# The first MLP's first chunk run for each token half apart, and the second half's norm queued behind the first half's products

## The chip, the cores and the metric

The kernel runs on one core of a Trainium2 chip. The metric is device microseconds (us) of one execution, as the median of several runs. In the profile PE is the matrix engine, PEld its weight load, DVE the vector engine, ACT the scalar engine, POOL the GpSimd engine, and SP the queue that issues the DMAs.

## What is computed

One inference step of two layers over 640 tokens of 1024 channels: 128 context tokens and 512 latent tokens. The part of the reference around the change, cut to what matters:

```python
xs = xs + m_lat[2] * ms                                      # token mixer's output, through w_out
hs = rmsnorm(xs, norm_mlp[i]) * (1.0 + m_lat[4]) + m_lat[3]   # norm and modulation
xs = xs + m_lat[5] * sqrelu_mlp(hs, mlp_w1[i], mlp_w2[i])     # square(relu(h @ w1)) @ w2, 1024 -> 4096 -> 1024
```

The context tokens take the same steps with their own modulation vectors. Layer 0 mixes tokens by a bidirectional linear recurrence, layer 1 by a convolution module (a matrix product with a gate, 31 taps along the tokens, a LayerNorm and another matrix product). The modulation vectors of a layer are one matrix product of a conditioning vector.

## The kernel before

**Layout.** Channels lie on the 128 partitions in eight tiles, tokens along the row. The tokens are worked in two halves of 320, called half 0 and half 1 here; the tiles of half 0 are `a` (input of a product) and `c` (hidden layer), those of half 1 `b` and `d`. Every operand is split in two parts (`h`, the rounded value, and `l`, the rest), and every product is made of three: `wh*ah` (L178), `wl*ah` (L181), `wh*al` (L182).

**Units.** A unit is one weight tile of 128 outputs and 1024 inputs against one half: 8 x 3 = 24 products into one PSUM tile `ps_mm`, of which there are three in turn (pool `mmp`, L79). For each weight tile `fetch` (L154) issues a DMA, an ACT cast (`wh`, L161) and a subtraction (`wl`, L163); line 162 says whether DVE or POOL does the subtraction, by the place of the tile in the list `plan`: POOL for the tiles of `w_out` and of the first MLP's chunk 0 and for a long stretch of layer 1, and in between (both_n to busy) POOL and DVE in turn. Weights are fetched three units ahead.

**The MLP.** The hidden layer of 4096 is worked in four chunks of 1024. `mlp_in` makes eight units and evacuates each by an ACT relu, a DVE multiplication (`hr`, L702), an ACT cast (`ch`, `dh`, L167) and a DVE subtraction (`cl`, `dl`, L168); `mlp_out` makes eight units whose results DVE adds to the residual stream `xr` (L285). The last product of the first `mlp_out` unit needs the last `cl` of the chunk.

**Background.** `bg` is a list of small steps of other work, each with a price in us; after every unit `between` (L193) hands out steps up to `budget[1]`. `drain` empties the list at once, or up to a mark. Two kinds of steps stand in it here. A norm of a half (L270): eight squares on ACT with DVE additions (`nacc`, L255), column sums on PE (`ps_n`, L236 or L228), the root and its inverse (`rc`, `rs`), a second set of PE products that spread it (L240), and eight times a multiplication (`nt`, L276), a modulation (L268 or ACT L266) and a split. And the 96 steps of layer 1's modulation (`mod_steps`, L115): 48 DMAs of 512 KB into three buffers `wm`, each read by two DVE instructions (`scratch`, L128) that multiply 1024 columns and sum them up.

**Order.** A scheduler puts the instructions of each engine in a fixed order, close to that of the code; an engine then works strictly through its own list. Before the change, the first MLP goes like this: `w_out` for half 0, then for half 1, with each half's norm queued behind it; `drain()` empties the list; then chunk 0 for both halves in groups of four units (32 units, budget 1.8), and chunks 1 to 3 for half 0 alone (48 units, budget 1.2), with the modulation steps behind them. What is called pass A here is that work of half 0. Pass B follows (L840 to L849): half 1's chunks 1 to 3, with the first matrix product of the convolution module for half 0 after five units, and the convolution of half 0 as background (budget 2.4). Then comes `pw2(0)`, the convolution module's last product for half 0, with half 1's next norm behind it.

Of the kernel before, what the change touches and what calls it, by code (L numbers as in the profile page):

```python
# [17 lines left out]
D = 1024  # L18
# [28 lines left out]
CA = 5  # L47
# [22 lines left out]
def hybrid_step(ctx: ExitStack, tc: tile.TileContext, xt, vec, pos, masks, ident_in, state, c_rows, w_mod0, w_modt,  # L70
# [25 lines left out]

# [1 line left out]
    mod = const.tile([P, 2, 48, 2], F32, name="mod")  # L98
    amod = const.tile([P, 2, 2, KT, 2], F32, name="amod")

    def mod_done(layer, j, src):
        """Adds the bias to chunks 2j and 2j+1, and for a chunk that scales makes norm_w * (1 + scale)."""
        bm = ap(vt, VEC["b_mod"].start + layer * 48 + j * 16, [[4, 4], [1, 4], [0, 2]])
        dst = ap(mod, (layer * 48 + j * 16) * 2, [[8, 4], [2, 4], [1, 2]])
        dve.tensor_tensor(dst, src, bm, ALU.add)
        for which in range(2):
            if j != (0, 2)[which]:
                continue
            base = (layer * 48 + (8, 32)[which]) * 2
            nw = VEC[("norm_mix", "norm_mlp")[which]].start + layer * 8  # L110
            dve.scalar_tensor_tensor(
                amod[:, layer, which].rearrange("p k s -> p (k s)"), ap(mod, base, [[1, 16]]), 1.0,
                ap(vt, nw, [[1, 8], [0, 2]]), ALU.add, ALU.mult)

    def mod_steps(cbs, raw_m, scratch, layer, j0, wm):  # L115
        """Chunks from 2 * j0 on of a layer's modulation, as dot products along rows of the transposed weights."""
        for s in range(2):
            cr = raw.tile([P, D], F32, tag="rw", name="cr")
            sync.dma_start(cr[:], c_rows[s:s + 1].partition_broadcast(P))
            act.activation(cbs[:, s], cr[:], AF.Sigmoid)  # L120
            dve.tensor_tensor(cbs[:, s], cbs[:, s], cr[:], ALU.mult)
        box = {}

        def step(i, s):
            if s == 0:
                box["w"] = wm()
                sync.dma_start(box["w"][:], w_modt[layer * 32 + i - 16 * (1 - layer)])
            tc.keep_in_program_order(dve.scalar_tensor_tensor(  # L128
                scratch, box["w"][:], 1.0, cbs[:, s], ALU.mult, ALU.mult, accum_out=raw_m[:, i, s:s + 1]))
            if s == 1 and i % 16 == 15:  # L130
                mod_done(layer, i // 16, ap(raw_m, (i - 15) * 2, [[8, 4], [2, 4], [1, 2]]))

        return [lambda i=i, q=q: step(i, q) for i in range(16 * j0, 48) for q in range(2)]
# [3 lines left out]

# [1 line left out]
    MLP = [[[w_mlp[l, c, u] for u in range(16)] for c in range(4)] for l in range(2)]  # L139
    PW1 = [w_pw1[u] for u in range(16)]  # L140
    PW2 = [w_pw2[u] for u in range(8)]
    plan = [w_in[u] for u in range(40)] + [w_out[u] for u in range(8)] * 2
    plan += MLP[0][0]
    both_n = len(plan)
    plan += MLP[0][1] + MLP[0][2] + MLP[0][3]
    busy = len(plan)
    plan += MLP[0][1][:CA] + PW1 + MLP[0][1][CA:] + MLP[0][2] + MLP[0][3] + PW2 + PW1
    plan += MLP[1][0] + MLP[1][1] + MLP[1][2] + PW2
# [59 lines left out]
    def linear(n, acts, evac, cols, group=8, after=between, u0=0, done=None):  # L208
        """n units of weights against the token halves given in cols: {half: (lo, hi)}."""
        first = pos_w[0]  # L210
# [11 lines left out]

# [1 line left out]
    def inv_rms(tp, acc, n, by_token):  # L224
        """1/rms of the columns of acc, the squares summed along D but for the partitions, on all partitions."""
        ps = axp.tile([P, 512], F32, tag="ax", name="ps_n")
# [17 lines left out]
    def rms_stat(tp, xs, n, by_token=False):  # L244
        """Steps that leave 1/rms over the KT tiles xs(k) in the returned box."""
        box = {}
# [53 lines left out]

# [1 line left out]
    h = {0: new_act("a"), 1: new_act("b")}  # L302
    first_ps = [[(mmp, "mm"), (scp, "sc")][half][0].tile([P, 512], F32, tag=("mm", "sc")[half], name=f"ps_f{half}")
                for half in (0, 1) for _ in range(3)]
    with tc.tile_pool(name="start", bufs=1) as st:
# [26 lines left out]

        # shift and scale in blocks of columns, so that the first products start with the first block
        wmb = {}
# [83 lines left out]
        sync.dma_start(vt[:, n0:], vec[:, n0:])  # L418
        # forget gate lower bounds: softmax over the layer axis, cumulated, less the first row
        lbt = const.tile([P, 16], F32, name="lbt")  # L420
# [40 lines left out]
    with tc.tile_pool(name="wm0", bufs=1) as wmp, tc.tile_pool(name="hd", bufs=1) as hd:  # L461
# [33 lines left out]
        def blocks(x, y, evac, w=SB, other=False):  # L495
            """Scores within blocks of w tokens (or across two neighbours), source token on the partition."""
            ps = scp.tile([P, 512], F32, tag="sc", name="ps_sc")
# [8 lines left out]
        def decay(hs, li):  # L506
            """Keeps the operands of a level aside and takes the running products one level up."""
            lv = LEVELS[li]
# [34 lines left out]
        def score(hs, li):  # L543
            """li < 0: equal tokens; else the pairs that part at that level."""
            if li < 0:
# [109 lines left out]

# [1 line left out]
    xpool = ctx.enter_context(tc.tile_pool(name="xpool", bufs=1))  # L657
# [37 lines left out]

# [1 line left out]
    def hid_evac(hid):  # L697
# [16 lines left out]
    def mlp_out(layer, cols, group=8, done=None):  # L714
        linear(8, hid, residual(xr, layer, 5), cols, group, done=done)

    def start_norm(layer, which, half, cols, first=True, by_token=False, on_dve=ND):
        """Queues a norm of one token half; returns its last step."""
        h[half] = new_act("ab"[half])
        steps = norm_steps(tp, xr, layer, which, h[half], *cols, by_token, on_dve)  # L720
        bg[:] = steps + bg if first else bg + steps
        return steps[-1]
# [4 lines left out]

    # w_out, then the first MLP; the first token half runs ahead of the second
    budget[1] = 3.0
    for cols in (A0, B0):  # L730
        linear(8, on, residual(xr, 0, 2), cols, done=lambda half: start_norm(0, 1, half, COLS[0][half], False, TM0, ND0))
    drain()
    with tc.tile_pool(name="wm1", bufs=1) as wmp:
# [3 lines left out]
            lambda: wmp.tile([P, D], F32, tag="wm", name="wm", bufs=3)))  # L737
        budget[1] = 1.8
        mlp_in(0, both, 4)
        mlp_out(0, both, 4)  # L740
        budget[1] = 1.2
        for c in (1, 2, 3):
            mlp_in(0, A0)
            mlp_out(0, A0)
# [100 lines left out]
    mlp_out(0, B0)  # L845
    for c in (2, 3):
        mlp_in(0, B0)
        mlp_out(0, B0)
# [118 lines left out]
```

## Time and profile before

| | |
|---|---|
| median of three runs | 1645.46 us (1644.57 to 1647.92) |
| span of the profiled execution | 1641.7 us, 3.8 us below that median |
| busy: PE, PEld | 1586.2 us (97%), 1542.8 us (94%) |
| busy: DVE, ACT, POOL | 1315.9 us (80%), 765.8 us (47%), 530.0 us (32%) |
| mean granted PE clock | 0.984 of full speed |
| chain that ended last | PE 61%, DVE 29%, ACT 4%, issue 3%, POOL 2% |
| HBM traffic | 145 GB/s over the span |

No time of the profiled execution other than its span is given. A share over the whole span mixes stages: PE is busy nearly throughout, but in which stretch DVE is nearly full as well has to be read from stretches of 5 to 30 us. PE's rows overlap, since a product is shown for 0.31 us and the next begins 0.147 us later; the distance of two starts is what a product costs.

### The profile page before, as it was taken

Reading aid. Unit: us, or ns where it says so; the run is one execution under the profiler, and the core shown is the slowest. Engines: PE = TensorE matmul, PEld = TensorE weight load, DVE = VectorE, ACT = ScalarE, POOL = GpSimd, SP = SyncE. Lnnn points to the kernel's source line nnn. Section 1 sums busy time; section 2 is a strip of 40 time slices with the busy share of each in tenths; the row PEclk is TensorE's granted clock in tenths of the full one; section 3 lists DMA queues with packets and bytes.
Section 4 is the critical chain, followed back from the end, with each engine's and each line's share of the span. In section 5 each row is a group of like instructions: output and inputs, shape, how many; then the busy total and the mean of one; then the engine's idle time right before and its main releaser. Section 6 shows DMA issues by size and latency. Waiting matters only on the chain.

```text
span 1641.7 us, 31432 instructions
## 1 busy us (share of the span) xinstructions
PE 1586.2 (97%) x12810; PEld 1542.8 (94%) x12810; DVE 1315.9 (80%) x2222; ACT 765.8 (47%) x1227; POOL 530.0 (32%) x257
## 2 busy tenths in 40 slices
PE   8999999999998999999999999999999899999997
PEld 7899999988898999999999999989999899999997
DVE  5788888878778998888989998999999767555544
ACT  3666655566355314334443435664344545334331
POOL 3100000002363423333666665567776520000000
PEclk8999999999998999999999999999999999999999
DMA  9333333334243566676444443334444344444411
GB/s 364 117 111 118 116 110 113 120 95 158 99 148 107 173 205 219 220 227 207 155 130 153 144 152 130 124 126 162 154 154 155 100 158 154 142 141 142 142 39 65
DMA packets 71296, 240.06 MB, mean 146 GB/s; under 512 B 7792, under 2 KB 14576, under 8 KB 70128
## 3 DMA queue, kind: packets, MB, share of 16 engines
q1 hardware_dynamic: 71152, 238.06, 43.7%
q8 instruction: 101, 1.65, 0.4%
q14 instruction: 43, 0.35, 0.1%
HBM read 234.36 MB, written 3.67 MB: 145 GB/s over the span
## 4 chain that ended last, share of the span: by engine, by line
PE 61%; DVE 29%; ACT 4%; issue 3%; POOL 2%; DMA 1%; SPq 0%; DVEq 0%; ACTq 0%; POOLq 0%
PE ps_mm L178 18%; PE ps_mm L182 18%; PE ps_mm L181 18%; DVE ps_cv L792 6%; DVE cl L168 3%; DVE scratch L128 3%; DVE nacc L255 2%; POOL wl L163 2%; DVE hr L702 2%; PE ps_sc L502 2%; DVE dl L168 1%; DVE wl L163 1%; DVE nt L276 1%; DVE nt L268 1%; ACT wh L161 1%
## 5 line engine op out<-in xcount | busy, mean ns | idle before, releaser
L163 POOL TENSOR_TENSOR wl<-rw,wh 128x1024 fp32r<-128x1024 f32 x202 | 504.2, 2502 | 754.7 <-ACT wh L161 705.2
L161 ACT CAST wh<-rw 128x1024 fp32r<-128x1024 f32 x334 | 348.4, 1046 | 314.5 <-PE ps_mm L182 220.8
L178 PE MATMUL ps_mm<-bh,wh 128*128 128x320 f32 (+1 forms) x1000 | 317.7, 318 | 2.9 <-DVE ub L770 1.6
L178 PE MATMUL ps_mm<-ah,wh 128*128 128x320 f32 (+1 forms) x1000 | 314.8, 315 | 4.6 <-DVE hr L702 2.7
L182 PE MATMUL ps_mm<-al,wh 128*128 128x320 f32 (+1 forms) x1000 | 310.8, 311 | 2.6 <-DVE al L168 2.6
L181 PE MATMUL ps_mm<-bh,wl 128*128 128x320 f32 (+1 forms) x1000 | 311.2, 311 | 0.0
L181 PE MATMUL ps_mm<-ah,wl 128*128 128x320 f32 (+1 forms) x1000 | 311.1, 311 | 0.0
L182 PE MATMUL ps_mm<-bl,wh 128*128 128x320 f32 (+1 forms) x1000 | 310.8, 311 | 0.0
L792 DVE SCALAR_TENSOR_TENSOR ps_cv<-ub,vt,ps_cv 128x319 f32<-128x319 f32 (+1 forms) x464 | 228.5, 553 | 0.4
L178 PEld LDWEIGHTS ps_mm<-ah,wh 128*128 128x128 f32 x1000 | 191.4, 191 | 9.8 <-issue 3.1
L182 PEld LDWEIGHTS ps_mm<-al,wh 128*128 128x128 f32 x1000 | 191.2, 191 | 4.0 <-DVE al L168 3.1
L181 PEld LDWEIGHTS ps_mm<-ah,wl 128*128 128x128 f32 x1000 | 191.4, 191 | 3.2 <-issue 2.6
L178 PEld LDWEIGHTS ps_mm<-bh,wh 128*128 128x128 f32 x1000 | 188.0, 188 | 5.8 <-DVE ub L770 1.9
L163 DVE TENSOR_TENSOR wl<-rw,wh 128x1024 fp32r<-128x1024 f32 x132 | 162.5, 1232 | 38.7 <-ACT wh L161 38.7
L181 PEld LDWEIGHTS ps_mm<-bh,wl 128*128 128x128 f32 x1000 | 187.9, 188 | 0.5
L182 PEld LDWEIGHTS ps_mm<-bl,wh 128*128 128x128 f32 x1000 | 188.1, 188 | 0.1
L182 PE MATMUL ps_mm<-dl,wh 128*128 128x320 f32 (+1 forms) x576 | 180.7, 314 | 2.4 <-DVE dl L168 2.4
L182 PE MATMUL ps_mm<-cl,wh 128*128 128x320 f32 (+1 forms) x576 | 177.5, 308 | 5.0 <-DVE cl L168 5.0
L178 PE MATMUL ps_mm<-dh,wh 128*128 128x320 f32 (+1 forms) x576 | 181.6, 315 | 0.0
L181 PE MATMUL ps_mm<-dh,wl 128*128 128x320 f32 (+1 forms) x576 | 180.2, 313 | 0.0
L178 PE MATMUL ps_mm<-ch,wh 128*128 128x320 f32 (+1 forms) x576 | 177.9, 309 | 0.4 <-ACT ch L167 0.4
L285 DVE SCALAR_TENSOR_TENSOR xr<-ps_mm,mod,xr 128x128 f32<-128x128 f32 (+2 forms) x240 | 97.4, 432 | 99.8 <-PE ps_mm L182 99.8
(209 smaller groups left out, 2625.4 us busy)
## 6 DMA issues: line engine op xcount, KB each, us to landing
rw<-in_w_mlp SPq DMA_DIRECT2D x230, 512.0 KB, 3.3
wm<-in_w_modt SPq DMA_DIRECT2D x80, 512.0 KB, 4.1
rw<-in_w_pw SPq DMA_DIRECT2D x48, 512.0 KB, 3.3
rw<-in_w_in SPq DMA_DIRECT2D x40, 512.0 KB, 3.5
wmb<-in_w_mod SPq DMA_DIRECT2D x8, 1024.0 KB, 10.1
rw<-in_w_out SPq DMA_DIRECT2D x16, 512.0 KB, 3.4
x<-in_xt SPq DMA_DIRECT2D x8, 320.0 KB, 5.5
xr<-in_xt SPq DMA_DIRECT2D x8, 320.0 KB, 5.8
```

Of the source, the lines that this page charges most:

```text
L128: tc.keep_in_program_order(dve.scalar_tensor_tensor(scratch, box["w"][:], 1.0, cbs[:, s], ALU.mult, ALU.mult, accum_out=raw_m[:, i, s:s + 1]))
L161: act.copy(wh[:], rw[:])
L163: eng.tensor_tensor(wl[:], rw[:], wh[:].bitcast(F32), ALU.subtract)
L168: eng.tensor_tensor(lo, src, hi.bitcast(F32), ALU.subtract)
L178: first = pe.matmul(ps[:, :n], wh[:, k, :], hi[:, :n], start=k == 0, stop=False)
L181: pe.matmul(ps[:, :n], wl[:, k, :], hi[:, :n], start=False, stop=False)
L182: pe.matmul(ps[:, :n], wh[:, k, :], lo[:, :n], start=False, stop=k == KT - 1)
L255: dve.tensor_tensor(box["acc"][:, :n], box["acc"][:, :n], t[:, :n], ALU.add)
L285: dve.scalar_tensor_tensor(x[:, u, a:b], ps[:, a - lo:b - lo], mvec(layer, chunk, u, s), x[:, u, a:b], ALU.mult, ALU.add)
L502: pe.matmul(ps[r:r + w, t * w:(t + 1) * w], x[:, s0:s0 + w], y[:, t0:t0 + w], start=True, stop=True, tile_position=(0, r))
L702: dve.tensor_tensor(r[:, :n], ps, r[:, :n], ALU.mult)
L792: dve.scalar_tensor_tensor(box[i][:, :m], u[:, j:j + m], w, box[i][:, :m], ALU.mult, ALU.add)
```

## The change

Chunk 0 of the first MLP is no longer run for both halves. Half 0 takes chunks 0 to 3 in pass A (64 units, budget 2.1 throughout), half 1 takes chunk 0 as the first of four chunks in pass B. The sixteen weight tiles of chunk 0 are therefore fetched and split twice. In pass A they now belong to the stretch in which POOL and DVE split in turn, in pass B POOL splits them. Of the two norms queued by `w_out`, only half 0's is emptied before the MLP begins; half 1's steps stay in `bg`, ahead of the modulation steps, and are handed out after the units of pass A. Comments and docstrings that were taken out move the line numbers of the changed kernel by one for most of the code.

```diff
-    plan += MLP[0][0]
     both_n = len(plan)
-    plan += MLP[0][1] + MLP[0][2] + MLP[0][3]
+    plan += MLP[0][0] + MLP[0][1] + MLP[0][2] + MLP[0][3]
     busy = len(plan)
-    plan += MLP[0][1][:CA] + PW1 + MLP[0][1][CA:] + MLP[0][2] + MLP[0][3] + PW2 + PW1
+    plan += MLP[0][0][:CA] + PW1 + MLP[0][0][CA:] + MLP[0][1] + MLP[0][2] + MLP[0][3] + PW2 + PW1
...
     budget[1] = 3.0
+    marks = {}
     for cols in (A0, B0):
-        linear(8, on, residual(xr, 0, 2), cols, done=lambda half: start_norm(0, 1, half, COLS[0][half], False, TM0, ND0))
-    drain()
+        linear(8, on, residual(xr, 0, 2), cols, done=lambda half: marks.update(
+            {half: start_norm(0, 1, half, COLS[0][half], False, TM0, ND0)}))
+    drain(marks[0])
...
-        budget[1] = 1.8
-        mlp_in(0, both, 4)
-        mlp_out(0, both, 4)
-        budget[1] = 1.2
-        for c in (1, 2, 3):
+        budget[1] = 2.1
+        for c in (0, 1, 2, 3):
             mlp_in(0, A0)
             mlp_out(0, A0)
...
-    for c in (2, 3):
+    for c in (1, 2, 3):
         mlp_in(0, B0)
         mlp_out(0, B0)
```

On PE, where the column sums of half 1's norm (L236, in the changed kernel L235) stand behind the last unit of `w_out`. Before, they stand in the middle of the first unit of the MLP, behind its first 14 products:

```order
L178 MATMUL ps_mm_6263<-ah_5771,wh_6058 128x320
L181 MATMUL ps_mm_6263<-ah_5771,wl_6059 128x320
L182 MATMUL ps_mm_6263<-al_5772,wh_6058 128x320
L178 MATMUL ps_mm_6263<-ah_5773,wh_6058 128x320
L181 MATMUL ps_mm_6263<-ah_5773,wl_6059 128x320
L236 MATMUL ps_n_6159<-ones_81,nacc_6136 80x1 x4
L182 MATMUL ps_mm_6263<-al_5774,wh_6058 128x320
```

Now they stand behind the second unit (`ps_mm_6222`) and ahead of the third (`ps_mm_6284`):

```order
L177 MATMUL ps_mm_6222<-ah_5779,wh_6090 128x320
L180 MATMUL ps_mm_6222<-ah_5779,wl_6091 128x320
L181 MATMUL ps_mm_6222<-al_5780,wh_6090 128x320
L235 MATMUL ps_n_6261<-ones_81,nacc_6202 80x1 x4
L177 MATMUL ps_mm_6284<-ah_5765,wh_6168 128x320
```

They moved from 14 to 48 products behind the end of `w_out`.

On DVE, what stands around the last additions of that norm (`nacc`). Before:

```order
L121 TENSOR_TENSOR cbs<-cbs,cr 128x1024
L285 SCALAR_TENSOR_TENSOR xr<-ps_mm,mod,xr 128x320
L168 TENSOR_TENSOR al<-nt,ah 128x320
L255 TENSOR_TENSOR nacc<-nacc,nsq 128x320
L285 SCALAR_TENSOR_TENSOR xr<-ps_mm,mod,xr 128x320
L255 TENSOR_TENSOR nacc<-nacc,nsq 128x320
L238 RECIPROCAL rc<-rc 80x4
```

and now:

```order
L284 SCALAR_TENSOR_TENSOR xr<-ps_mm,mod,xr 128x320
L162 TENSOR_TENSOR wl<-rw,wh 128x1024
L167 TENSOR_TENSOR al<-nt,ah 128x320
L254 TENSOR_TENSOR nacc<-nacc,nsq 128x320 x2
L284 SCALAR_TENSOR_TENSOR xr<-ps_mm,mod,xr 128x320
L254 TENSOR_TENSOR nacc<-nacc,nsq 128x320
L162 TENSOR_TENSOR wl<-rw,wh 128x1024
L254 TENSOR_TENSOR nacc<-nacc,nsq 128x320 x3
L701 TENSOR_TENSOR hr<-ps_mm,hr 128x320
```

Three subtractions of weights (`wl`, two of them in these rows) now stand ahead of the norm's last addition, where there were none.

On DVE, the beginning of chunk 1's `mlp_in` for half 0, in pass A. Before:

```order
L702 TENSOR_TENSOR hr<-ps_mm,hr 128x320
L168 TENSOR_TENSOR cl<-hr,ch 128x320
L128 SCALAR_TENSOR_TENSOR scratch,raw_m<-wm,cbs 128x1024
L702 TENSOR_TENSOR hr<-ps_mm,hr 128x320
L163 TENSOR_TENSOR wl<-rw,wh 128x1024
L168 TENSOR_TENSOR cl<-hr,ch 128x320
L128 SCALAR_TENSOR_TENSOR scratch,raw_m<-wm,cbs 128x1024
```

and now:

```order
L701 TENSOR_TENSOR hr<-ps_mm,hr 128x320
L128 SCALAR_TENSOR_TENSOR scratch,raw_m<-wm,cbs 128x1024
L167 TENSOR_TENSOR cl<-hr,ch 128x320
L128 SCALAR_TENSOR_TENSOR scratch,raw_m<-wm,cbs 128x1024 x2
L701 TENSOR_TENSOR hr<-ps_mm,hr 128x320
L162 TENSOR_TENSOR wl<-rw,wh 128x1024
L167 TENSOR_TENSOR cl<-hr,ch 128x320
L128 SCALAR_TENSOR_TENSOR scratch,raw_m<-wm,cbs 128x1024
```

Before, one modulation step goes with each unit, 8 in the eight units of a `mlp_in`; now it is 13 in a `mlp_in` and 15 in a `mlp_out`.

## Rows read from the trace of the kernel before

**Rows 1.** Timeline of PE, 496 to 520: start, duration, instruction, idle time before.

```profile
497.61 0.31 PE L178 MATMUL ps_mm<-ah,wh 128*128 128x320 f32 x1
...
499.52 0.31 PE L181 MATMUL ps_mm<-ah,wl 128*128 128x320 f32 x1
507.41 1.22 PE L236 MATMUL ps_n<-ones,nacc 128*80 128x1 f32 x8 [7.59 <-DVE nacc L255]
...
508.91 0.47 PE L178 MATMUL ps_mm<-ah,wh 128*128 128x320 f32 x1
...
512.11 0.47 PE L178 MATMUL ps_mm<-ah,wh 128*128 128x320 f32 x1
```

**Rows 2.** Timeline of DVE, 488 to 520.

```profile
505.80 1.56 DVE L255 TENSOR_TENSOR nacc<-nacc,nsq 128x320 f32<-128x320 f32 x1 [0.54 <-ACT nsq L254]
```

**Rows 3.** Timeline of POOL, 470 to 560.

```profile
488.45 5.01 POOL L163 TENSOR_TENSOR wl<-rw,wh 128x1024 fp32r<-128x1024 f32 x2 [4.66 <-ACT wh L161]
498.57 8.43 POOL L163 TENSOR_TENSOR wl<-rw,wh 128x1024 fp32r<-128x1024 f32 x3 [5.11 <-ACT wh L161]
```

**Rows 4.** Waits of PE, whole span: waiting instruction, releaser, total, times, longest.

```profile
PE ps_mm L178 <- DVE hr L702: 2.7, 1, 2.7
```

**Rows 5.** Stretches: time, busy PE, PEld, DVE, ACT, POOL, granted PE clock, DMA.

```profile
545.00:550.00 5.00, 2.68 (x10) 2.68 (x11) 4.47 (x9) 0.94 (x3) 0.37 (x1) 0.66 0.68 210
550.00:555.00 5.00, 5.00 (x25) 5.00 (x24) 4.47 (x9) 1.55 (x4) 0.00 (x0) 0.65 0.53 188
...
1050.00:1055.00 5.00, 4.22 (x18) 4.06 (x19) 2.26 (x6) 3.55 (x5) 5.00 (x3) 0.68 0.61 201
```

**Rows 6.** Timeline of DVE, 646 to 690: `mlp_in`, then `mlp_out`, of chunk 1.

```profile
649.77 1.21 DVE L128 SCALAR_TENSOR_TENSOR scratch<-wm,cbs 128x1024 f32<-128x1024 f32 x1
...
650.91 0.48 DVE L702 TENSOR_TENSOR hr<-ps_mm,hr 128x320 f32<-128x320 f32 x1
651.32 1.21 DVE L163 TENSOR_TENSOR wl<-rw,wh 128x1024 fp32r<-128x1024 f32 x1
652.45 0.48 DVE L168 TENSOR_TENSOR cl<-hr,ch 128x320 fp32r<-128x320 f32 x1
652.85 1.21 DVE L128 SCALAR_TENSOR_TENSOR scratch<-wm,cbs 128x1024 f32<-128x1024 f32 x1
...
655.00 1.87 DVE L168 TENSOR_TENSOR cl<-hr,ch 128x320 fp32r<-128x320 f32 x1 [0.53 <-ACT ch L167]
...
661.03 0.66 DVE L285 SCALAR_TENSOR_TENSOR xr<-ps_mm,mod,xr 128x128 f32<-128x128 f32 x2
661.62 1.21 DVE L128 SCALAR_TENSOR_TENSOR scratch<-wm,cbs 128x1024 f32<-128x1024 f32 x1
```

**Rows 7.** Timeline of POOL, 646 to 690.

```profile
654.12 2.41 POOL L163 TENSOR_TENSOR wl<-rw,wh 128x1024 fp32r<-128x1024 f32 x1 [4.62 <-DVE scratch L128]
661.60 3.50 POOL L163 TENSOR_TENSOR wl<-rw,wh 128x1024 fp32r<-128x1024 f32 x1 [5.07 <-ACT wh L161]
```

**Rows 8.** Groups on DVE, 690 to 717 (chunk 2, `mlp_in`): busy, mean ns, idle before.

```profile
L168 DVE TENSOR_TENSOR cl<-hr,ch 128x320 fp32r<-128x320 f32 x8 | 10.1, 1260 | 2.4 <-ACT ch L167 2.4
```

**Rows 9.** Groups on DVE, 718 to 745 (chunk 2, `mlp_out`).

```profile
L128 DVE SCALAR_TENSOR_TENSOR scratch<-wm,cbs 128x1024 f32<-128x1024 f32 x9 | 11.3, 1253 | 0.0
L285 DVE SCALAR_TENSOR_TENSOR xr<-ps_mm,mod,xr 128x128 f32<-128x128 f32 (+1 forms) x16 | 5.4, 379 | 7.6 <-PE ps_mm L182 7.6
```

**Rows 10.** Groups on DVE and POOL, 570 to 600 (chunk 0, mostly `mlp_out`).

```profile
L128 DVE SCALAR_TENSOR_TENSOR scratch<-wm,cbs 128x1024 f32<-128x1024 f32 x14 | 22.9, 1638 | 0.2
...
L163 POOL TENSOR_TENSOR wl<-rw,wh 128x1024 fp32r<-128x1024 f32 x5 | 13.4, 2676 | 18.3 <-ACT wh L161 18.3
```

**Rows 11.** Timeline of PE, 655 to 665 and 1046 to 1057.

```profile
660.02 0.42 PE L182 MATMUL ps_mm<-cl,wh 128*128 128x320 f32 x1 [0.48 <-DVE cl L168]
...
1050.78 0.81 PE L228 MATMUL ps_n<-nacc,ones 128*128 128x320 f32 x2 [3.23 <-DVE nacc L255]
```

**Rows 12.** Timeline of DVE, 1000 to 1060 (end of pass B, `pw2(0)`).

```profile
1043.14 7.59 DVE L255 TENSOR_TENSOR nacc<-nacc,nsq 128x320 f32<-128x320 f32 x3 [0.34 <-ACT nsq L254]
```

## The prediction

> **What bounds the kernel now.** I read the page's busy shares first, then the waits of PE, then PE and DVE in stretches, and at last single rows of DVE and POOL in the stretches that the change touches. The busy shares (in the table) say that PE is the bound: 97% of the span. The reader should see two things beyond that. First, where the remaining PE time goes around the change: 7.59 us at 499.8, waiting for the last addition (`nacc`) of half 1's norm [rows 1]; 2.70 us at 544.6, where a product waits for a PSUM tile that DVE has not yet read (`hr`) [rows 4]; 0.48 us at 659.5, the last `cl` of a chunk, which occurs three times in pass A; and 3.23 us at 1047.6, another norm in `pw2(0)` [rows 11]. After waits of 2.7 us and more the granted clock shows half speed for a while: 0.66, 0.65 and 0.68 in three such stretches [rows 5], that is products at 1.2 instead of 2.4 GHz. In rows: 13 products from 497.61 to 499.52 cost 0.147 us each, 12 from 508.91 to 512.11 cost 0.267 [rows 1]. The short waits of 0.48 us have no such tail.
>
> Second, DVE is not idle enough in pass A to be left out. In `mlp_in` of chunk 1 its rows follow each other without a gap, but for waits of 0.53 us on ACT [rows 6]; in `mlp_out` it has slack, 7.6 us in 27 us of waiting for PE [rows 9]. And POOL and DVE take turns. The `cl` at 655.00 needs 1.87 us instead of 0.48 [rows 6], while POOL's subtraction of 654.12 to 656.53 runs; the subtraction at 661.60 needs 3.50 instead of 2.41 us [rows 7], while DVE's `scratch` runs. Over a `mlp_in`, eight `cl` have a mean of 1.260 us against 0.48 for a free one [rows 6, 8]: 6.2 us lost, to four POOL subtractions (every other of eight tiles), so b = 1.56 us of DVE time for each.
>
> PE's products are the same in number and size before and after. So the time changes by what PE waits and by what it runs at half clock, nothing else. I add that up piece by piece.
>
> **1. The norm's wait at 499.8.** Now 7.59 us, and 14 products at half clock, 14 x (0.267 - 0.147) = 1.7: 9.3 us. The change puts the column sums 48 instead of 14 products behind `w_out`, so PE arrives at 497.6 + 48 x 0.147 = 504.7. The last addition ends at 507.4 now [rows 2]. The order puts three `wl` of 1.13 us ahead of it [rows 6], +3.4; but of the five POOL subtractions in that time [rows 3] half go to DVE, and 2.5 x 1.56 = 3.9 us of blocking with them. So it is ready at about 506.9, and PE waits 2.2 us, perhaps again with the half clock (1.7). Left: about 4; **saved 5.3**. Bounds: no wait at all, 9.3 saved; no relief from POOL, 6.1 us of wait and the clock, 1.5 saved.
>
> **2. Pass A.** This is the main term. Norm steps of half 1 and three `wl` fill DVE for the first five or six units of chunk 0, about as long as PE takes; I count no loss. From there to the middle of chunk 3's `mlp_out` stand all 96 modulation steps, in 54 units instead of 80 before. From start to start in the rows a `scratch` costs 1.14 us, a `wl` 1.13, `hr` 0.41, `cl` 0.40, the two `xr` of a unit 0.59 [rows 6]. For eight units PE needs 8 x 24 x 0.147 = 28.2 us. DVE needs
> - in a `mlp_in`: 13 x 1.14 + 4 x 1.13 + 8 x 0.81 = 25.8, and two waits on ACT of 0.53, 26.9 in all;
> - in a `mlp_out`: 15 x 1.14 + 4 x 1.13 + 8 x 0.59 = 26.3;
>
> each with four POOL subtractions, 4b. DVE then sets the pace: a `mlp_in` takes 4b - 1.3 longer than PE, a `mlp_out` 4b - 1.9. PE can run ahead by its three PSUM tiles only, and at each end of `mlp_in` it must wait for the last `cl`, so the lag reaches PE there in full. Three of each (the `mlp_out` of chunks 0 to 2, the `mlp_in` of chunks 1 to 3) make 24b - 9.6. The last `mlp_out` has half the steps, and DVE catches up.
>
> How large is b when DVE has no slack? The `mlp_in` rows say 1.56. The `mlp_out` of chunk 2 says nearly nothing: 9 `scratch` at 1.253 instead of 1.21 us [rows 6, 9], but there DVE was idle for 7.6 us, and POOL could run then. In chunk 0, where two modulation steps went with a unit, 14 `scratch` at 1.638 us lost 6.0 us to five subtractions [rows 10]: 1.2 each, without what other instructions lost. After the change all of pass A looks like that or like `mlp_in`. I take 1.56: **27.8 us lost**. From below: where the two strictly take turns, the instructions that take part (`scratch`, `wl`, `cl` and POOL's own 2.41 us) need 14.8 + 4.5 + 3.2 + 9.6 = 32.1 in a `mlp_in` and 17.1 + 4.5 + 9.6 = 31.2 in a `mlp_out`, even if `hr` and `xr` hide entirely: 3 x 3.9 + 3 x 3.0 = 20.7. From above: all of 2.41 us lost each time, 48.
>
> The Trainium skill has a rule for this (SBUF — State Buffer, section "Who interferes with whom"): a DVE instruction with two inputs in SBUF and a GpSimd instruction that reads SBUF exclude each other, and the one that issues second is blocked until the other ends. The 1.87 and 3.50 us rows agree, one in each direction. By that rule the loss is not under the 20.7 us of turns, and a pass A at PE's pace is ruled out.
>
> **3. Half clock after the new waits.** The lag of a chunk, some 9 us, shows partly as short waits for PSUM and mostly at the end of `mlp_in`, where PE has no product left to run ahead with. I expect three waits over 2.7 us, each with about 14 products at half clock as at 508.9, 3 x 1.7 = **5.1 lost**: DVE stands then too, since its next rows wait for PE. Bounds 0 (lag spread in short waits) and 8.
>
> **4. What pass A no longer has.** The wait at 544.6 (2.70) with the half clock behind it: from 545 to 555 PE made 35 products in 7.7 busy us [rows 5], where 52 would fit, so 17 x 0.147 = 2.5. And the three waits of 0.48, which are inside DVE's pace now: **6.6 saved**.
>
> **5. `pw2(0)`.** In pass B the convolution's 59 units of background are followed by 16 units that have none, so its LayerNorm no longer shares `pw2(0)` with half 1's norm; on DVE only the three additions that need 7.59 us now [rows 12] and the residual stay, and the column sums have 48 products' time. The wait of 3.23 and its 1.7 of half clock: **4.9 saved** (bounds 2 and 4.9).
>
> **At nothing:** 16 more DMAs of 512 KB and 16 more ACT casts; in the stretches shown the queue moves 188 to 210 GB/s and ACT is busy under 1.6 us in 5 at chunk 0 [rows 5], and a DVE-paced pass gives both more time, not less. If that cover failed, a late weight would show as a PE wait for `wl`, some us. The eight more POOL subtractions in pass B run beside 56 us of PE time that has no convolution steps beside it. The wait of half 0's next norm at the start of pass B keeps its place relative to PE, and its price.
>
> **Sum.** -5.3 + 27.8 + 5.1 - 6.6 - 4.9 = +16.1. On the profiled execution 1641.7 becomes 1657.8; with the 3.8 us between its span and the median, 1645.5 becomes **1661.6**.
>
> **Rivals.**
> - *PE keeps the pace (faster than before).* If POOL does the waiting and DVE is hardly held up, b under 0.3 us, pass A loses nothing and the savings are left: 1645.5 - 5.3 - 6.6 - 4.9 = 1628.7. It is faster than before from 24b - 9.6 = 16.8, b = 1.1, down (0.9 with the half clock). For it: the 3.50 us row and chunk 2's `mlp_out`. Against: `mlp_in` at 1.56 and chunk 0 at 1.2. Between 0.7 and 1.1, with less saved at the norm, the result is within 0.2% of before. The Trainium skill's page "Perfetto Trace Analysis" (section "Identifying the Most-Contended Engine") would point here: the engine with the highest occupancy is the one to look at, and that is PE with 97%. The rows of pass A speak against taking that share for every stretch.
> - *DVE loses more.* b of 2.0, the norm's wait as long as before less the 34 products (1.5 saved), and half clock in every chunk: -1.5 + 38.4 + 8 - 6.6 - 4 = +34.3, 1680.
> - *The change doesn't do what it says:* the norm's wait stays, only later in PE's list. That is the 1.5 us bound of step 1; alone it makes 1665.
>
> **How the numbers follow.** Forecast, 1650 to 1676: 0.69. PE keeps the pace, or nearly: 0.10. Within 3.3 us of before (0.2%, about what a measurement of this kernel can tell from no change): 0.09. Above 1676: 0.12. The range of 1647 to 1679 leaves about 0.12 below and 0.08 above. Faster 0.10, same 0.09, slower 0.81.
>
> **What would show it.** Right: in pass A of the changed kernel DVE busy nearly without a gap, near 95%, where PE falls below 90%; waits of PE for `cl` and `hr` of several us at three ends of `mlp_in`, with a granted clock under 0.8 behind them; 64 units from the end of `w_out` in about 258 us instead of 226; a wait of PE for `nacc` of 0 to 4 us; none of 3.2 in `pw2(0)`. Wrong: DVE rows of `cl` and `scratch` in pass A near their free 0.48 and 1.21 us while POOL's grow; PE at 70 products in 10 us throughout pass A; or PE waiting there for weights and not for DVE's evacuations.

## The result

The changed kernel takes **1668.85 us** (median of four runs, 1666.87 to 1671.74); the kernel before, with one more run on the same chip, 1646.66 us (1644.57 to 1647.92). The ratio is 1.0141, with a 95% interval of 1.0126 to 1.0156: **22.2 us slower**, of which the forecast of 1661.6 had 16.1.

| | before | after |
|---|---|---|
| span of the profiled execution | 1641.7 us | 1670.0 us |
| busy PE | 1586.2 us (97%) | 1597.7 us (96%) |
| busy DVE | 1315.9 us (80%) | 1352.2 us (81%) |
| busy POOL | 530.0 us (32%) | 546.7 us (33%) |
| mean granted PE clock | 0.984 | 0.979 |

The two spans differ by 28.3 us, more than the medians, because the two profiled executions don't lie in the middle of theirs: after, it is the slowest of the four (1671.74 us, with a span of 1670.0), and before, a span of 1641.7 us lies below the fastest of the four timed runs, also with those 1.7 us added. What is compared below are pieces inside the spans.

**Where the time went.** The first MLP begins with the first product on `ah`, and pass B begins with the first on `bh`. On the timeline of PE these are, for the kernel after:

```profile
499.49 0.31 PE L177 MATMUL ps_mm<-ah,wh 128*128 128x320 f32 x1
...
773.58 0.31 PE L177 MATMUL ps_mm<-bh,wh 128*128 128x320 f32 x1
```

and for the kernel before, where the MLP's beginning is the first row of [rows 1]:

```profile
799.27 0.31 PE L178 MATMUL ps_mm<-bh,wh 128*128 128x320 f32 x1
```

After: 274.09 us for 64 units. Before: 301.66 us for 80 units; without the 16 units of half 1 that have moved (16 x 24 x 0.1468 = 56.4), 245.3. The pass has become **28.8 us longer**. From the start of pass B to the end of the wait for `nt` behind `pw2(0)`, 274.72 us before and 327.82 after, less the same 56.4, it has become **3.3 us shorter**. That makes 25.5; 1.9 us of the rest is there already when the MLP begins (499.49 against 497.61; in the runs e1 to e4 below it begins between 496.84 and 498.64). Another 0.9 us lies elsewhere and is not placed.

The views of the pass. First its stretches (time, busy PE, PEld, DVE, ACT, POOL, granted PE clock, DMA share, GB/s):

```profile
530.00:540.00 10.00, 6.11 (x37) 5.36 (x36) 10.00 (x17) 3.59 (x7) 3.32 (x1) 0.97 0.52 159
...
600.00:610.00 10.00, 4.38 (x20) 3.51 (x19) 9.97 (x17) 2.72 (x5) 3.06 (x1) 0.71 0.72 245
640.00:650.00 10.00, 9.20 (x63) 8.93 (x62) 9.44 (x16) 3.12 (x5) 2.52 (x1) 1.00 0.74 238
670.00:680.00 10.00, 4.17 (x18) 3.40 (x17) 9.97 (x17) 3.04 (x5) 2.56 (x1) 0.80 0.72 234
...
740.00:750.00 10.00, 4.76 (x17) 4.25 (x18) 9.97 (x16) 2.81 (x5) 2.29 (x2) 0.71 0.70 249
```

DVE is busy 94 to 100% in each; PE is at 42 to 61% in four of them. Over the whole span DVE's share rose by one point only; it is the stretches that tell. Then the waits of PE over the whole span (instruction, releaser, total, times, longest), where before the longest in this pass were 7.59 and 2.7 [rows 1, 4]:

```profile
PE ps_mm L177 <- ACT ch L166: 15.1, 9, 2.9
PE ps_mm L181 <- DVE cl L167: 10.7, 8, 2.3
PE ps_mm L177 <- DVE hr L701: 6.8, 8, 1.0
```

And PE's timeline at the ends of `mlp_in` of chunks 1 to 3, with the norm's column sums (L235) as the first row:

```profile
507.81 0.73 PE L235 MATMUL ps_n<-ones,nacc 128*80 128x1 f32 x8 [0.77 <-DVE nacc L254]
...
605.21 0.63 PE L181 MATMUL ps_mm<-cl,wh 128*128 128x320 f32 x1 [2.26 <-DVE cl L167]
...
674.11 0.41 PE L181 MATMUL ps_mm<-cl,wh 128*128 128x320 f32 x1 [2.26 <-DVE cl L167]
677.42 0.63 PE L177 MATMUL ps_mm<-ch,wh 128*128 128x320 f32 x1 [2.89 <-ACT ch L166]
677.85 0.47 PE L180 MATMUL ps_mm<-ch,wl 128*128 128x320 f32 x1
678.11 0.47 PE L177 MATMUL ps_mm<-ch,wh 128*128 128x320 f32 x1
...
742.91 0.41 PE L181 MATMUL ps_mm<-cl,wh 128*128 128x320 f32 x1 [2.26 <-DVE cl L167]
```

The norm's wait is 0.77 us where it was 7.59. In its place stand, once per chunk, a wait for the last `cl` and behind it one for `ch`, whose ACT cast waits in turn for DVE's `hr`. Behind them products start 0.26 to 0.27 us apart (677.85, 678.11): half clock, for 11 to 20 products at each of four such places. From one `cl` wait to the next it is 68.9 and 68.8 us (605.21, 674.11, 742.91); before, 57.14 (660.02 [rows 11] to the same row at 717.16).

Last, one such chunk on DVE and POOL by groups, 606 to 675:

```profile
L128 DVE SCALAR_TENSOR_TENSOR scratch<-wm,cbs 128x1024 f32<-128x1024 f32 x29 | 48.4, 1668 | 0.1
L162 DVE TENSOR_TENSOR wl<-rw,wh 128x1024 fp32r<-128x1024 f32 x8 | 11.9, 1492 | 0.0
L167 DVE TENSOR_TENSOR cl<-hr,ch 128x320 fp32r<-128x320 f32 x8 | 3.9, 484 | 0.5 <-ACT ch L166 0.5
```

```profile
L162 POOL TENSOR_TENSOR wl<-rw,wh 128x1024 fp32r<-128x1024 f32 x8 | 23.0, 2880 | 45.9 <-ACT wh L160 42.3 <-DMA rw<-in_w_mlp 3.6
```

Before, `cl` was blocked and `scratch` mostly free [rows 6, 8]; now `cl` is free (484 ns) and `scratch` and `wl` pay: 29 x (1.668 - 1.216) + 8 x (1.492 - 1.217) = 15.3 us for eight POOL subtractions, so **b = 1.91 us**. The free durations are those of the run `e2_split_dve` below, without POOL. One such loss on POOL and on DVE, to be read beside [rows 6, 7]:

```profile
669.51 3.06 POOL L162 TENSOR_TENSOR wl<-rw,wh 128x1024 fp32r<-128x1024 f32 x1 [4.89 <-ACT wh L160]
```

```profile
670.26 0.48 DVE L701 TENSOR_TENSOR hr<-ps_mm,hr 128x320 f32<-128x320 f32 x1
670.67 2.97 DVE L128 SCALAR_TENSOR_TENSOR scratch<-wm,cbs 128x1024 f32<-128x1024 f32 x1
```

POOL's row is longer than its free 2.41 us because a `scratch` was running when it began; then it runs beside `hr`, and the next `scratch` takes 2.97 us instead of 1.22.

### The profile page after: what moved, and what is told of

It reads as the page before. It is cut to its first block, busy times and chain, and to the rows that moved or that the text cites. A ratio compares the mean times of both kernels' runs of the same rounds, so it can differ in the third digit from the quotient of the medians.

```text
span 1670.0 us, 31559 instructions
## 1 busy us (share of the span) xinstructions
PE 1597.7 (96%) x12810; PEld 1547.4 (93%) x12810; DVE 1352.2 (81%) x2230; ACT 780.7 (47%) x1243; POOL 546.7 (33%) x265
## 5 line engine op out<-in xcount | busy, mean ns | idle before, releaser
L162 POOL TENSOR_TENSOR wl<-rw,wh 128x1024 fp32r<-128x1024 f32 x210 | 520.2, 2483 | 761.4 <-ACT wh L160 752.1
L160 ACT CAST wh<-rw 128x1024 fp32r<-128x1024 f32 x350 | 365.1, 1047 | 311.0 <-PE ps_mm L181 208.7
L162 DVE TENSOR_TENSOR wl<-rw,wh 128x1024 fp32r<-128x1024 f32 x140 | 180.2, 1289 | 38.5 <-ACT wh L160 38.4
L177 PE MATMUL ps_mm<-ch,wh 128*128 128x320 f32 (+1 forms) x576 | 182.3, 317 | 17.1 <-ACT ch L166 15.1
L180 PE MATMUL ps_mm<-ch,wl 128*128 128x320 f32 (+1 forms) x576 | 180.3, 313 | 0.0
```

What stands on the lines that cost most here:

```text
L160: act.copy(wh[:], rw[:])
L162: eng.tensor_tensor(wl[:], rw[:], wh[:].bitcast(F32), ALU.subtract)
L177: first = pe.matmul(ps[:, :n], wh[:, k, :], hi[:, :n], start=k == 0, stop=False)
L180: pe.matmul(ps[:, :n], wl[:, k, :], hi[:, :n], start=False, stop=False)
```

## The experiments

The last column is the length of the piece from the MLP's first product to pass B's first, from the same two rows of PE's timeline in each run. Differences of it are of single executions; the ratio is against the kernel before on the same chip. That kernel's median was 1644.33 to 1646.66 us on the chips used, so differences of two medians from the table are good to some 2 us.

| run | starts from | median us | ratio, 95% | MLP to pass B, us |
|---|---|---|---|---|
| before | | 1646.66 | | 301.66 (80 units) |
| after | | 1668.85 | 1.0126 to 1.0156 | 274.09 |
| e1_norms_drained | after | 1680.54 | 1.0199 to 1.0233 | 286.29 |
| e2_split_dve | after | 1644.98 | 0.9989 to 1.0011 | 249.07 |
| e3_split_pool | after | 1705.89 | 1.0353 to 1.0399 | 311.29 |
| e4_half_mod | after | 1630.31 | 0.9891 to 0.9925 | 234.21 |
| e5_before_norm_bg | before | 1642.96 | 0.9983 to 1.0001 | 300.81 (80 units) |
| e6_early_dve | after | 1646.46 | 0.9998 to 1.0023 | 229.21 |
| e7_before_split_dve | before | 1627.60 | 0.9879 to 0.9911 | 286.85 (80 units) |
| e8_chunk0_dve | before | 1632.33 | 0.9903 to 0.9930 | 290.47 (80 units) |

### Pass A without POOL, and with POOL alone

Two runs change only who subtracts the weights of pass A. First, DVE does all of them:

```diff
-            eng = pool if i in (0, 2) or 40 <= i < both_n or busy <= i < calm or (both_n <= i < busy and i % 2) else dve
+            eng = pool if i in (0, 2) or 40 <= i < both_n or busy <= i < calm else dve
```

> The changed kernel, with all weight subtractions of pass A on DVE and none on POOL: 51 instead of 26 among the modulation steps. Theory (what DVE loses is blocking by POOL, about 2 us for each POOL subtraction, more than the 1.13 us that DVE needs itself): a mlp_in needs 13 x 1.14 + 8 x 1.13 + 8 x 0.81 + 1 = 31.3, a mlp_out 15 x 1.14 + 8 x 1.13 + 8 x 0.59 = 30.9, a chunk 62 instead of 68.9 us; cl and scratch at their free 0.48 and 1.21 us; over some 3.3 chunks 22 us faster than the changed kernel, about 1647. Rival (DVE has simply too much to do, and POOL takes work off it): 25 more subtractions of 1.13 us, 28 us slower, 1697.

Measured: 1644.98, some 24 us faster than after and equal to before, near the theory's 1647, although DVE was given 32 more subtractions. The groups of one chunk on DVE, 656 to 720:

```profile
L128 DVE SCALAR_TENSOR_TENSOR scratch<-wm,cbs 128x1024 f32<-128x1024 f32 x29 | 35.3, 1216 | 0.0
L162 DVE TENSOR_TENSOR wl<-rw,wh 128x1024 fp32r<-128x1024 f32 x16 | 19.5, 1217 | 0.0
```

The same 29 `scratch` take 35.3 us instead of 48.4. From chunk to chunk it is 64.0 us, where the theory had 62. The waits for `cl` are gone; small ones for `wl`, 12.0 us in all, the longest 2.1, stand in their place: DVE still sets the pace.

Second, POOL does all of them:

```diff
-            eng = pool if i in (0, 2) or 40 <= i < both_n or busy <= i < calm or (both_n <= i < busy and i % 2) else dve
+            eng = pool if i in (0, 2) or 40 <= i < calm else dve
```

> The changed kernel, with all weight subtractions of pass A on POOL and none on DVE. Theory (the two take turns; POOL's 2.41 us block more than DVE's 1.13): by turns alone 14.8 + 3.2 + 8 x 2.41 = 37.3 in a mlp_in and 17.1 + 19.3 = 36.4 in a mlp_out, 74 a chunk instead of 68.9, 16 us slower than the changed kernel, about 1685; with 2 us of blocking for each, 76 a chunk and about 1693. Rival (DVE's own work is what counts): 26 x 1.13 = 29 us less on DVE, and some 25 us faster, about 1643.

Measured: 1705.89, 37 us slower than after; the direction is the theory's, the size above it. DVE by groups, 624 to 703, one chunk:

```profile
L128 DVE SCALAR_TENSOR_TENSOR scratch<-wm,cbs 128x1024 f32<-128x1024 f32 x28 | 60.4, 2156 | 0.3
L167 DVE TENSOR_TENSOR cl<-hr,ch 128x320 fp32r<-128x320 f32 x9 | 7.8, 867 | 3.9 <-ACT ch L166 3.9
```

28 x (2.156 - 1.216) + 9 x (0.867 - 0.487) = 29.7 us for 16 POOL subtractions: b = 1.86, the same as with eight. Most of the rest of the 79.0 us per chunk is DVE's own waiting for the ACT cast `ch`, 3.9 us, which the expectation had not counted.

### Half of the modulation work

Of the two `scratch` instructions that read each buffer `wm`, the second is left out, and with it the modulation of the latent tokens, which stays at zero (a `memset` of POOL, not shown here, sets it so):

```diff
-            tc.keep_in_program_order(dve.scalar_tensor_tensor(
-                scratch, box["w"][:], 1.0, cbs[:, s], ALU.mult, ALU.mult, accum_out=raw_m[:, i, s:s + 1]))
+            if layer == 0 or s == 0:
+                tc.keep_in_program_order(dve.scalar_tensor_tensor(
+                    scratch, box["w"][:], 1.0, cbs[:, s], ALU.mult, ALU.mult, accum_out=raw_m[:, i, s:s + 1]))
```

> The changed kernel without the DVE instruction of every second modulation step: layer 1's modulation is computed for the context tokens only and left at zero for the latent ones, with all DMAs and all prices as they were. Theory (DVE's work sets the pace of pass A, and the modulation steps are what fills it): 7 of 13 steps in a mlp_in, 26 to 28 us with blocking against PE's 28.2, so pass A runs at PE's pace, the waits at the ends of mlp_in are under 1 us, and the time is about 40 us below the changed kernel, 1627 to 1632. Rival (the extra fetches, casts and weights of chunk 0, or the clock, are what costs): they are all still there, and the time stays within 5 us of 1669.

Measured: 1630.31, 38.5 us faster than after, as expected. The stretch 660 to 680, with POOL at work as in the kernel after:

```profile
660.00:680.00 20.00, 20.00 (x139) 20.00 (x138) 12.14 (x24) 5.83 (x7) 8.09 (x3) 1.00 0.89 298
```

PE is at its full pace at full clock with POOL subtracting beside it. So it isn't POOL's work by itself that costs time, and not the 298 GB/s of DMA either: it is DVE's load, and POOL's work where DVE has no time to spare. The piece takes 234.2 us, 9 more than 64 units at full pace (225.4).

### The norm, emptied at once as before

```diff
-    drain(marks[0])
+    drain()
```

> The changed kernel, but with both norms emptied before the MLP begins, as in the kernel before; chunk 0 stays apart. In its order the column sums of half 1's norm stand 22 products behind w_out, so PE waits some 5 to 6 us there again, with 1.7 us of half clock, against 1.5 us in the changed kernel. Theory (DVE sets the pace from about 505 us to the end of pass A): DVE has the same list to work off, only in another order, so what PE waits more at the norm it waits less in pass A, and the time is that of the changed kernel, 1668.9, within 3 us. Rival (the norm's wait is a saving of its own, as step 1 of the prediction has it): 7.8 us slower, 1676 to 1678.

Measured: 1680.54, 12 us slower than after. That is against the theory, and more than the rival's 7.8. PE's waits, and DVE's, at the norm:

```profile
504.91 1.23 PE L235 MATMUL ps_n<-ones,nacc 128*80 128x1 f32 x8 [4.55 <-DVE nacc L254]
...
531.97 0.64 PE L177 MATMUL ps_mm<-ah,wh 128*128 128x320 f32 x1 [2.92 <-DVE hr L701]
...
535.79 0.63 PE L180 MATMUL ps_mm<-ah,wl 128*128 128x320 f32 x1 [3.19 <-DVE wl L162]
```

```profile
506.47 0.17 DVE L237 RECIPROCAL rc<-rc 80x4 f32<-80x4 f32 x1 [1.61 <-ACT rc L236]
507.39 0.49 DVE L701 TENSOR_TENSOR hr<-ps_mm,hr 128x320 f32<-128x320 f32 x1 [0.74 <-ACT hr L700]
...
511.74 0.88 DVE L275 TENSOR_TENSOR nt<-xr,ps_n 128x320 f32<-128x320 f32 x2 [3.87 <-PE ps_n L239]
```

The theory said that the norm's wait is off the path where DVE sets the pace. But the emptied norm makes DVE itself stand, 1.61 + 0.74 + 3.87 = 6.2 us, because its next rows wait for ACT and for PE's slow products; in the kernel after it stands 1.3 us there. From the last `cl` of the first `mlp_in` on, the two kernels take equally long, so the remaining 7 us lie in the first `mlp_in` too. There `wl` stand in the list behind `scratch`, and PE waits for one (3.19); whether that is all of it is open.

### The norm part alone

On the kernel before, chunk 0 still for both halves, but half 1's norm behind half 0's first units. The budget of chunks 1 to 3 goes from 1.2 to 1.3 as well, which the diff here leaves out:

```diff
-    drain()
+    drain(marks[0])
...
+        budget[1] = 2.7
+        mlp_in(0, both, 4, n=4)
         budget[1] = 1.8
-        mlp_in(0, both, 4)
+        mlp_in(0, both, 4, u0=4, n=4)
```

> The kernel before, with the norm part of the change alone: chunk 0 is still run for both halves, but the list is emptied only up to half 0's norm, and half 1's norm is handed out after the first four units of half 0. Theory: the 9.3 us of the norm's wait and half clock go, but DVE has next to no room in chunk 0 of the kernel before (26.87 busy of 27 us from 518 to 545, 27.27 of 28 from 575 to 603), so that what DVE had done while PE waited must be done there at PE's cost; -2 to -5 us against before, 1639.5 to 1642.5. Rival: the norm is an independent saving of 7 to 9 us, 1635.5 to 1637.5. Against both: chunk 0 is DVE-paced and gives all of it back, within 1 us of before.

Measured: 1642.96, a ratio of 0.9983 to 1.0001: no gain that stands out, nearest to the third possibility; the low end of the theory, 2 us, lies inside the interval too. PE's timeline:

```profile
507.54 0.42 PE L182 MATMUL ps_mm<-al,wh 128*128 128x320 f32 x1 [2.10 <-DVE al L168]
...
568.70 0.41 PE L178 MATMUL ps_mm<-ch,wh 128*128 128x320 f32 x1 [1.59 <-DVE hr L702]
...
574.58 0.41 PE L178 MATMUL ps_mm<-ch,wh 128*128 128x320 f32 x1 [2.06 <-DVE hr L702]
```

The 7.59 us are gone, and their half clock. Back come 2.10 + 0.51 + 0.35 at 501 to 508 with 14 products at half clock (1.7), and new waits of 1.59, 2.06, 0.70 and 0.54 from 549 to 582: 9.6 us for the 9.3 that were saved. The work that DVE does now beside PE had been done while PE waited, and there was no room for it elsewhere. The wait that was 2.70 us is 1.99 here, without half clock behind it, and with the larger budget two waits for `ch` are new, 1.04 and 0.66 us in chunks 2 and 3; so the run is not the norm part alone.

### Where before loses time: POOL beside chunk 0

The kernel before, with the weights of chunk 0 and of pass A on DVE:

```diff
-            eng = pool if i in (0, 2) or 40 <= i < both_n or busy <= i < calm or (both_n <= i < busy and i % 2) else dve
+            eng = pool if i in (0, 2) or 40 <= i < 56 or busy <= i < calm else dve
```

> The kernel before with all weights of the first MLP's chunk 0 and of pass A subtracted on DVE, none on POOL. Theory: POOL's subtractions cost time only where DVE sets the pace. In chunks 1 to 3 of the kernel before PE does, so nothing changes there but the three waits of 0.48 us; in chunk 0, where DVE has no room, 16 subtractions of 1.13 us take the place of 16 blockings of 1.2 to 1.6 us: together -7 to +1 us against before, 1637.5 to 1645.5. Rival: blocking by POOL costs PE time in any stretch, and moving the subtractions gives the 24 us here too, near 1621; or DVE is overfull in chunk 0, and the 16 subtractions add 10 us or more, 1655.

Measured: **1627.60, 1.05% faster than before** (interval 0.89 to 1.21%), the fastest kernel here that computes everything. That lies between what theory and rival said. PE's timeline at the norm:

```profile
498.90 0.31 PE L178 MATMUL ps_mm<-ah,wh 128*128 128x320 f32 x1
...
504.08 0.37 PE L236 MATMUL ps_n<-ones,nacc 128*80 128x1 f32 x3 [0.62 <-DVE nacc L255]
```

The norm's wait, the thing that the change goes after, falls to 0.62 us although the norm is still emptied at once. These are DVE rows ahead of it in the kernel before:

```profile
489.31 1.90 DVE L168 TENSOR_TENSOR al<-nt,ah 128x320 fp32r<-128x320 f32 x1
491.13 2.71 DVE L268 TENSOR_SCALAR nt<-nt,amod,mod 128x128 f32<-128x128 f32 x2
...
500.92 1.34 DVE L168 TENSOR_TENSOR al<-nt,ah 128x320 fp32r<-128x320 f32 x1 [0.76 <-ACT ah L167]
502.18 2.62 DVE L255 TENSOR_TENSOR nacc<-nacc,nsq 128x320 f32<-128x320 f32 x1
```

Against 0.48 for a free `al` or `nacc` and 0.63 for a free pair of `nt`, these four and the last `nacc` of 1.56 [rows 2] lose 1.42 + 2.08 + 0.86 + 2.14 + 1.08 = 7.6 us to the five POOL subtractions of [rows 3]. That is as much as the whole wait of 7.59 us. The run doesn't show it to be the only cause, though. With the weights moved, the scheduler also put the column sums 30 products behind `w_out` instead of 14: 16 x 0.147 = 2.35 us of PE's time. The last addition ended 9.75 us behind the MLP's first product before (497.61, [rows 1, 2]) and ends 5.1 behind it here (498.90), although four weight subtractions now stand ahead of it on DVE:

```profile
503.54 0.49 DVE L255 TENSOR_TENSOR nacc<-nacc,nsq 128x320 f32<-128x320 f32 x1
```

So 4.6 of the 7.0 us by which the wait fell come from DVE being done earlier, with POOL off its rows, and 2.35 from the place of the column sums. The norm's place counts too, but for the smaller part.

With chunk 0's sixteen weights alone on DVE and chunks 1 to 3 as before:

```diff
-            eng = pool if i in (0, 2) or 40 <= i < both_n or busy <= i < calm or (both_n <= i < busy and i % 2) else dve
+            eng = pool if i in (0, 2) or 40 <= i < 56 or busy <= i < calm or (both_n <= i < busy and i % 2) else dve
```

> The kernel before with the sixteen weights of chunk 0 alone subtracted on DVE; in chunks 1 to 3 POOL and DVE take turns as before. The run with all of them on DVE was 16.8 us faster than before, and its trace shows the norm's wait at 503.46 down to 0.62 us, no half clock at 545, and the three waits of 0.48 us gone. Theory: POOL's subtractions cost nothing where PE sets the pace (chunks 1 to 3), so all but some 1.5 us of the 16.8 come from chunk 0 and the norm beside it: -15 us, 1628 to 1631 against 1644. Rival: a third of it or more comes from the 24 subtractions in chunks 1 to 3: -11 us or less, 1633 or more.

Measured: 1632.33, 13.8 us faster than before (11.5 to 16.0 by the interval): by time alone between theory and rival. The trace decides. Chunk 1 to chunk 2, by the first product of each, is 57.18 us here and 56.43 where DVE does all; three chunks make 2.2 us for 24 POOL subtractions that stand where PE sets the pace (the waits of 0.48 are back, 649.03 is one). Chunk 1 took 57.15 us in the kernel before too, so all of this run's gain, 11.2 us between the two rows of the table, comes from chunk 0 and the norm, whose column sums stand 30 products behind `w_out` in this run as well:

```profile
503.07 0.30 PE L236 MATMUL ps_n<-ones,nacc 128*80 128x1 f32 x2 [0.71 <-DVE nacc L255]
...
649.03 0.42 PE L182 MATMUL ps_mm<-cl,wh 128*128 128x320 f32 x1 [0.48 <-DVE cl L168]
```

### Modulation steps ahead of the pass

The kernel after, pass A on DVE, and 16 modulation steps handed out beside `w_out`:

```diff
+        early = [(1.2, f) for f in mod_steps(
...
-        budget[1] = 2.1
+        bg.extend(early[:16])
+        for cols in (A0, B0):
+            linear(8, on, residual(xr, 0, 2), cols, done=lambda half: marks.update(
+                {half: start_norm(0, 1, half, COLS[0][half], False, TM0, ND0)}))
+        drain(marks[0])
+        bg.extend(early[16:])
+        budget[1] = 1.8
```

> The changed kernel with all weights of pass A subtracted on DVE, and with 16 of the 96 modulation steps handed out beside w_out, ahead of pass A (DVE was busy 13 to 14 of 20 us there in the kernel before, from 440 to 480); budget 1.8 in pass A instead of 2.1. Theory: pass A is DVE-paced, so 16 steps of 1.14 to 1.21 us less there give up to 18 to 19 us, less what PE had no loss from; against the changed kernel with all of pass A on DVE (1645) -10 to -15 us: 1630 to 1635. Rival: w_out has POOL's subtractions beside it, so that the steps cost PE there what they save later, 1640 to 1645.

Measured: 1646.46, which is the rival's. Pass A is now at PE's pace, 229.21 us with one wait of 0.50, 19.9 less than without the early steps. But `w_out`, where POOL still subtracts, pays all of it; PE's timeline there:

```profile
464.69 0.61 PE L177 MATMUL ps_mm<-ch,wh 128*128 128x320 f32 x1 [4.08 <-DVE xr L284]
...
480.53 0.46 PE L177 MATMUL ps_mm<-dh,wh 128*128 128x320 f32 x1 [2.44 <-DVE xr L284]
...
492.30 0.96 PE L235 MATMUL ps_n<-ones,nacc 128*80 128x1 f32 x6 [6.48 <-DVE nacc L254]
```

With a fourth of 0.42 these are 13.4 us, and 50 products at half clock, 50 x 0.12 = 6.0: 19.4 us. From 441 to 492 DVE's rows took 19.6 us longer in all than free ones, beside eleven POOL subtractions, and the sixteen steps themselves are 18.2 us of work for DVE. No run takes POOL off `w_out` as well, so how much of the 19.4 is which stays open. What the run shows is that a place beside POOL gave nothing.

## Why the prediction came out as it did

The mechanism held: with 96 modulation steps in 54 units instead of 80, DVE sets the pace of pass A, and POOL's subtractions raise the price. Against PE's full pace (225.4 us for 64 units) the pass after loses 48.7 us. Halving the steps leaves 8.8 of it (e4); taking POOL out leaves 23.7 (e2), and taking POOL and 16 steps out leaves 3.8 (e6, inside the pass). The signs came as said: from 530 to 770 DVE is busy 237.4 of 240 us and PE 210.1, and behind the long waits the granted clock is 0.71 to 0.80. The sign and the range held with it. The forecast of the change was 6 us low, and by its own pieces the pass went +28.8 instead of +21.0, and `pw2(0)` -3.3 instead of -4.9. The 258 us that the prediction named as a sign for the pass don't follow from its sum, which gives 245.3 + 21.0 = 266.3; measured are 274.09.

**Step 1, the norm: right in kind, better than said.** Forecast 5.3 saved, with about 4 left. Measured: waits of 0.77 (`nacc`) and 0.70 (the spreading product, for `rc`), no half clock, so 7.8 saved. The last addition came about 1 us earlier than worked out, and PE arrived 0.4 us later. As a gain of its own, though, this term was doubtful: on the kernel before, nearly the same part brings 0.9 us in the trace (e5), while on the kernel after, emptying the norm costs 12 (e1).

**Step 2, pass A: the term that was mis-sized, by b.** b was taken as 1.56, from a `mlp_in` where DVE's rows had no gap but short waits for ACT [rows 6, 8]; measured it is 1.91 with eight POOL subtractions per chunk, 1.86 with sixteen. The formula around it stands. DVE needs 26.9 + 26.3 + 8 x 1.91 = 68.5 us per chunk; the trace has 68.9. With b = 1.91, 24b - 9.6 is 36.2 instead of 27.8: +8.4. The prediction took b over into a pass with less slack, and b grew as the slack went. In the `mlp_in` of before each POOL subtraction runs beside an `hr`, which isn't held up, and beside DVE's wait of 0.53 us for ACT [rows 6, 7], so 0.85 of its 2.41 us costs nothing. After, a `scratch` stands between `hr` and `cl`; the wait for ACT is mostly gone, and of 2.41 us only the time of an `hr` or `xr` costs nothing (the rows at 669.51 to 670.67): 79% are lost.

**Step 3, half clock: not a cost of its own.** Forecast 5.1 on top of step 2. The three clusters were there, and a fourth. But from the wait at 536.34 to that at 742.91, three periods, the pass lost 37.5 us against PE's full pace, of which 36.2 is step 2. Only 1.3 is left. In the chunk shown above DVE stands idle 0.6 us in 69, so it never waited for the slow products: PE ran them in time that it would have waited anyway. "DVE stands then too" was the false sentence. It becomes true when the slow stretch does reach DVE, as at the drained norm (3.87 in e1).

**Counted at nothing, and not nothing.** From 742.91 to the end of the pass, where DVE was to catch up, PE lost 5.9 us: the wait of 2.89 for `ch`, 15 products at half clock (1.8) and small ones. The head of the pass, up to 536.34, lost 5.3 us, with a `cl` wait of 1.77 that had no price; the sum had left 4 there for the norm and 3.9 of losses of before that it didn't touch (the norm's own products among them), so it ended 2.6 better. Together 8.4 - 3.8 + 5.9 - 2.6 = 7.9, which is the difference between +21.0 and +28.8. That the total came nearer than its largest errors is luck: within the pass, 14.3 us were too low and 6.4 too high.

**Step 4** stands as it was: the waits of before in this pass, 2.70 and the three of 0.48, went into DVE's pace. **Step 5** was 1.6 too large: the 3.23 and its half clock are gone, but pass B has one more end of `mlp_in`, with a wait of its own, which the change's description shows and the sum left out:

```profile
1047.79 0.41 PE L181 MATMUL ps_mm<-dl,wh 128*128 128x320 f32 x1 [0.96 <-DVE dl L167]
```

The rest of step 5 is 0.6 us more in the wait for `nt` behind `pw2(0)` (1.56 against 1.00).

**The rivals.** That PE keeps the pace needed b under 1.1. It fell with the first view of stretches. "DVE loses more" had b nearly right, at 2.0, and was wrong in the half clock and the norm. "The change doesn't do what it says" fell with the wait of 0.77. (PE's 97% there is the share of its matmul rows, which overlap; its weight loads, 94%, name the same engine.)

**How much of it is POOL.** With chunk 0 and pass A on DVE in both kernels the change costs nearly as much: 1644.98 against 1627.60, 17 us. DVE then needs 64.0 us per chunk where PE needs 56.4 (by the formula it would be 53.2 + 8 x 1.13 = 62.2). Between the MLP's first product and pass B, e2 loses 23.7 us against PE's full pace and e7 5.0, a difference of 18.7. So the first cause is the density of the steps, and what POOL adds to the price of the change is the difference between 22 and 17. On the kernel before POOL costs nearly as much, 16.8 us, but mostly in another place, chunk 0 and its norm, and there with the shifted column sums in it. Not tried: moving a third of the steps into pass B.

## What to carry to other kernels

Price a moved piece of background work in the stretch that receives it: per chunk, add up the time of the engine that does it, with its blocking by others, and compare that with the bound engine's, before anything is counted for the wait that goes away. A wait at a place is not yet a fault of the place alone; here the blocked rows ahead of the norm added up to as much as PE's wait, and one line that took POOL off that stretch won 16.8 us where the rearrangement lost 22. A loss per blocked instruction, read where the blocked engine has slack, was a lower bound here for where it has none (1.56 against 1.91).

## What the runs showed of the hardware

A DVE instruction loses most of the length of each POOL subtraction once DVE is full: 1.86 to 1.91 of 2.41 us, whether every other weight is POOL's or all are; in chunks 1 to 3 of the kernel before, where PE sets the pace, the whole price on the path was 2.2 us for 24 of them, 0.09 each. So a subtraction that takes DVE 1.13 us itself was cheaper there than on POOL (-24 us for 32 of them moved to DVE, +37 us for 32 moved to POOL). Blocked were the instructions with two inputs in SBUF (`scratch`, `wl`, `cl`, `al`, `nacc`), as the prediction's rule says, and also `nt`, a multiplication and addition with one wide input: 2.71 us for a pair instead of 0.63 in the row at 491.13. The Trainium skill names that kind too (SBUF — State Buffer, section "Who interferes with whom"): `tensor_scalar` can enter modes that use both of DVE's port pairs, one of which it shares with GpSimd, and can then contend with it; the row agrees. `hr` and `xr`, which read one input from PSUM, kept 0.48 and 0.34 to 0.41 us throughout, also in a chunk where sixteen POOL subtractions ran.
